# Modulation accumulated by one VectorE instruction per block, row norms with only the power on GpSimd

## Chip, core and metric

The kernel runs on one core of a Trainium2 chip. A core has a TensorE (PE in the profile, with its weight loads as PEld), a VectorE (DVE), a ScalarE (ACT), a GpSimd (POOL), and a SyncE (SP) that here issues nearly all DMAs. Each engine runs its own instructions in order and waits for the others at semaphores. The metric is the time of one execution in microseconds (us). Besides the reported time, the profile of one execution gives its span, from the first to the last instruction.

## The reference, cut to what matters

A sequence of 512 rows of width 1024, in float32, passes through two transformer blocks of two layers each. What the change touches in the second block is the norm around every sublayer and the modulation of that norm by a vector `c`:

```python
def rms_norm_2(x, g): x * rsqrt(mean(x*x) + 1e-6) * g

def sandwich(x, c_act, sublayer, g_pre, g_post, w_mod, b_mod):
    shift, scale, gate = split(c_act @ w_mod + b_mod, 3)      # w_mod is 1024 x 3072
    h = rms_norm_2(x, g_pre) * (1 + scale) + shift
    return x + gate * rms_norm_2(sublayer(h), g_post)
```

`sandwich` is applied four times (even mixer, MLP, odd mixer, MLP). The modulation `c_act @ w_mod` doesn't depend on `x`, so it can be computed at any time before its first use.

## The kernel before

Rows lie on 128 partitions, as four tiles (t = 0 to 3) of 128 rows. Dense products are taken in three fp32r matmuls each, high part by high part, low by high, high by low. For that every weight block of 128x1024 is split when it has arrived: ACT writes `whi`, DVE writes `wlo` = `raw` - `whi`. Activations are turned on TensorE (products with `ident`) and split likewise into `fTh` (ACT) and `fTl` (DVE); the `fT` of a layer is what its first dense products read. Results land in eight PSUM banks (`bank`).

One program order per engine is written out by a planner in the kernel: class `Line` keeps a clock per engine with estimated costs, and `defer` puts a piece of work into a heap until the planner's clock says that its inputs are there. TensorE's own stream is written in the same pass, so where a matmul stands in TensorE's order depends on when the planner reckons its inputs ready. A matmul whose inputs come later than reckoned holds up all that stand behind it.

Three places matter here.

**The modulation** (`mod_open`, `mod_load`, `mod_step`, `mod_go`, `mod_finish`) is computed inside the convolution FFN of both layers of the first block. There are 12 sums (4 sublayers, 3 kinds), 6 in each layer, and each is built from 8 blocks of 128x1024 weights (`mraw`, loaded by SP). The first block of a sum is scaled by `cact` into `macc` on ACT. Each of the other 7 was scaled in place on ACT and added to `macc` on GpSimd. Then four short products with `ones` on TensorE sum `macc` over the partitions. Steps are handed out along the up projections, one or two for each block of up weights.

**The norms between sublayers.** `post_start` and `out_part` finish a sublayer: sum of squares on ACT, `rstd` on GpSimd (a multiply-add with the mean and epsilon, then a power of -0.5), and on DVE `xr` = `y` * `rstd` + `xr`. Then `pre` squares `xr` on ACT, takes `rstd` on GpSimd, and on DVE multiplies by `rstd` and `scB` and adds `shB`; the result is turned into the next `fT`. `ln_pre_start` is the same hand-over after the last FFN of the first block. There are four hand-overs with `pre`, of four tiles each, and four ends with `post_start`.

**The start**: `hybrid` loads the gate bias `bg` and halves it on DVE before anything else of the layer.

In the profile every instruction has the line of the helper that records it (L186), so rows are told apart by their tiles.

Of the kernel before, what the change touches and what calls it, by code (L numbers as in the profile page):

```python
# [12 lines left out]
F32 = mybir.dt.float32  # L13
# [290 lines left out]
class KB:  # L304
# [305 lines left out]
    def split(self, hi, lo, ps, scale=None):  # L610
# [5 lines left out]
        else:  # L616
            nc.scalar.activation(hi, ps, AF.Copy, scale=scale)
            nc.vector.scalar_tensor_tensor(lo, ps, scale, hi.bitcast(F32), op0=ALU.mult, op1=ALU.subtract)

    def rstd(self, var, n, mul, eps, tag="rstd", pool=False):  # L620

        nc = self.nc
        ve = self.small(n, tag + "v")
        if mul == 1.0:
            nc.vector.tensor_scalar_add(ve, var, eps)
        else:
            (nc.gpsimd if pool else nc.vector).tensor_scalar(ve, var, mul, eps, op0=ALU.mult, op1=ALU.add)
        r = self.small(n, tag)
        nc.gpsimd.tensor_tensor(r, ve, self.mhalf[:, :n], op=ALU.pow)
        return r  # L630
# [62 lines left out]
    def setup(self):  # L693
        nc, A = self.nc, self.A
        self.ident = self.cn.tile([P, P], F32, name="ident")
        if not self.planning:
            make_identity(self.tc.nc, self.ident)
        self.mhalf = self.cn.tile([P, 64], F32, name="mhalf")
        nc.vector.memset(self.mhalf, -0.5)
        self.xd = A["x"]  # L700

    def first_x(self):
# [62 lines left out]
    def probs_out(self, pool, u):  # L765


        nc, sh = self.nc, u.shared
        if not sh:
            sh["pt"] = [self.tile(pool, (P, u.wide // P, 2, P), f"pt{e}") for e in range(2)]  # L770
            sh["ev"] = Event(2, lambda: self.defer(0, pv, *sh["pt"]))
        for e in range(2):
            pp = self.ps((P, 4, P))
            self.transpose4(pp, [u.sc[e][:, b * P:b * P + P] for b in range(u.nkb)])
            pt = sh["pt"][e][:, :u.nkb, u.pr, :]
            if e == 0:
                nc.scalar.activation(pt, pp[:, :u.nkb, :], AF.Copy)
            else:
                nc.vector.tensor_copy(pt, pp[:, :u.nkb, :])
        u.read.set()  # L780

        def pv():
            po = self.ps((P, 2 * P))
            vc = slice(64 * u.kv, 64 * u.kv + 64)
            for b in range(u.nkb):
                for e in range(2):
                    nc.tensor.matmul(po[64 * e:64 * e + 64, :], lhsT=u.v[:, u.b0 + b, vc],
                                     rhs=sh["pt"][e][:, b, :, :].rearrange("p r q -> p (r q)"),
                                     start=b == 0, stop=b == u.nkb - 1)
            self.poll()  # L790
            sl, k = slice(u.i * P, u.i * P + P), 2 * u.kv
            self.split(u.br.h[:, k:k + 2, sl], u.br.l[:, k:k + 2, sl], po.rearrange("p (r q) -> p r q", r=2))

        sh["ev"].set()

# [55 lines left out]
    def launch(self, pool, unit, step, br, **kw):  # L851


        units, depth = [], kw["bufs"] // 2

        def start(n):
            if n >= depth and not units[n - depth].read.done:
                units[n - depth].read.after(lambda: self.defer(0, lambda: start(n)))
                return
            unit(pool, units[n])  # L860

        for n in range(16):
            kv, i, pr = n // 8, n // 2 % 4, n % 2
            u = Unit(kv=kv, i=i, pr=pr, shared={} if pr == 0 else units[-1].shared, br=br, read=Event(),
                     **{k: v for k, v in kw.items() if k != "band"})
            u.b0, u.nkb, u.add = kw["band"](i)
            units.append(u)
            self.defer(n * step, lambda n=n: start(n), kw["kh"], kw["kl"])


    def hybrid(self, l, xT):
        nc, A = self.nc, self.A
        with self.pool("hp") as hp:
            W = Weights(self, "w_in", l)
            WB = Weights(self, "w_branch", l)
            bg = self.load(hp, A["b_gate"][l], (P, 24), "bg")
            nc.vector.tensor_scalar_mul(bg, bg, 0.5)
            mg = self.tile(hp, (P, KD, S), "mg")

            def branch(n, br, first, done=None):  # L880
# [20 lines left out]
            brc = new_br()  # L901
            with self.pool("cp") as cp:
                self.branch_c(cp, l, xT, W, brc)
                self.flush()
            bra = new_br()
            with self.pool("ap") as ap, ExitStack() as es:
# [361 lines left out]
    def mod_open(self, pool, end):  # L1268
        self.mod_pool, self.mod_raw, self.mod_end = pool, {}, end
        self.mod_left = Event((end - self.mod_n) // KD)  # L1270
        for j in range(2):
            self.mod_load(self.mod_n + j)

    def mod_load(self, i):
        if i < self.mod_end:
            s, kind, k = self.mod_steps[i]
            raw = self.tile(self.mod_pool, (P, D), "mraw", 3)
            o = (kind * KD + k) * P * D
            self.nc.sync.dma_start(raw, self.A["mod_w"][s][o:o + P * D].rearrange("(p c) -> p c", p=P))
            self.mod_raw[i] = raw  # L1280
# [8 lines left out]
    def mod_go(self):  # L1289
        nc, i = self.nc, self.mod_todo[0]  # L1290
        if not self.planning and nc.ready(self.mod_raw[i]) > self.now():
            self.defer(0, self.mod_go, self.mod_raw[i])
            return
        self.mod_todo.pop(0)
        s, kind, k = self.mod_steps[i]
        self.mod_load(i + 2)
        raw = self.mod_raw.pop(i)
        ck = self.cact[:, k:k + 1]
        if k == 0:
            self.mod_acc = self.tile(self.mod_pool, (P, D), "macc", 2)  # L1300
            nc.scalar.activation(self.mod_acc, raw, AF.Copy, scale=ck)
        else:
            nc.scalar.activation(raw, raw, AF.Copy, scale=ck)
            nc.gpsimd.tensor_tensor(self.mod_acc, self.mod_acc, raw, op=ALU.add)
        if k == KD - 1:
            acc, row = self.mod_acc, self.mod_sums[kind][s]

            def sums():
                ps = self.ps()
                for j in range(4):  # L1310
                    self.mm(ps[32 * j:32 * j + 32, 0:256], self.ones[:, 0:32], acc[:, 256 * j:256 * j + 256], 256)
                r = self.tile(self.mod_pool, (P, 256), "msum", 2)
                nc.scalar.activation(r, ps[:, 0:256], AF.Copy)
                nc.sync.dma_start(row.rearrange("(j c) -> j c", j=4), r[0:128:32, :])
                if c_last:
                    self.mod_finish(self.mod_pool)
                self.mod_left.set()

            c_last = i == len(self.mod_steps) - 1
            self.defer(0, sums, acc)  # L1320
# [12 lines left out]


    def open_pre(self, pool, s):
        self.shB = self.bcast(pool, self.mod_rows[0][s], D, "shB", 1, self.nc.sync)
        self.scB = self.bcast(pool, self.mod_rows[1][s], D, "scB", 1, self.nc.sync)

    def pre(self, t, x, h, fT, done=None):

        nc, scB, shB = self.nc, self.scB, self.shB
        ss = self.small(1, "ss1")
        nc.scalar.activation(h, x, AF.Square, accum_out=ss)

        def root():
            r = self.rstd(ss, 1, 1.0 / D, RMS_EPS, pool=True)
            self.defer(0, lambda: scale(r), r)

        def scale(r):
            nc.vector.scalar_tensor_tensor(h, x, r, scB, op0=ALU.mult, op1=ALU.mult)  # L1350
            nc.vector.tensor_tensor(h, h, shB, op=ALU.add)
            if done:
                done.set()
            self.defer_turn(t, h, fT)

        self.defer(0, root, ss)

    def open_post(self, s):
        bp = self.open_right()
# [4 lines left out]
    def out_part(self, t, n, ps, first, last):  # L1364
# [6 lines left out]
            nc.vector.tensor_tensor(y, y, ps, op=ALU.add)  # L1371
        if last:
            ss, gB = self.yss[:, t, n:n + 1], self.gB[:, 512 * n:512 * n + 512]
            nc.scalar.activation(ps, y, AF.Square, accum_out=ss)
            self.defer(0, lambda: nc.vector.tensor_tensor(y, y, gB, op=ALU.mult), ss)

    def post_start(self, s, out):
# [19 lines left out]
        def after(t):  # L1397
            if t > 1:
                self.wait(scaled[t - 2], True)
            y, xr = y4[:, t, :], xrs[t]  # L1400
            ss = self.small(1, "ss1")
            nc.vector.tensor_tensor(ss, self.yss[:, t, 0:1], self.yss[:, t, 1:2], op=ALU.add)
            r = self.rstd(ss, 1, 1.0 / D, RMS_EPS, pool=True)

            def scale():
                nc.vector.scalar_tensor_tensor(xr, y, r, xr, op0=ALU.mult, op1=ALU.add)
# [329 lines left out]
    def diff(self, dp, hT, W, v, yT):  # L1736
        nc, A = self.nc, self.A
        sub = self.load(dp, A["e_diff_norm"], (P, 1), "sub")
        nc.vector.tensor_scalar_mul(sub, sub, 1.0 - LAM_INIT)

        def head(h):
            T = self.tile(dp, (P, 512), "T", 2)
            self.toeplitz(T, h, 0, 512)
            qk = []
            shared = {}

            def unit(i):
# [3 lines left out]
                for m in range(2):  # L1751
# [3 lines left out]
                    nc.vector.tensor_tensor_reduce(s, ps[:, :Wd], T[:, 384 - i * P:512], 1.0, NEG,  # L1755
                                                   ALU.add, ALU.max, mx[:, m:m + 1])
                    s2.append(s)
                nc.vector.tensor_scalar_mul(nm_, mx, -1.0)
                for m in range(2):
                    nc.scalar.activation(s2[m], s2[m], AF.Exp, bias=nm_[:, m:m + 1], accum_out=sums[:, m:m + 1])  # L1760
# [49 lines left out]
            def ev(i, ps):  # L1810
                t = self.tile(dp, (P, 2, S), f"qk{i}", 2, F32R)
                qk.append(t)
                if i == 0:
                    self.stack_q([t[:, e, :] for e in range(2)], ps, HD ** -0.5)
                else:
                    qk.append(self.tile(dp, (P, 2, S), "qkl", 1, F32R))
                    self.stack_k(t, qk[2], ps)
                    for n in range(NT):
# [295 lines left out]
```

## Time and profile before

| | |
|---|---|
| median of 3 runs | 3478.86 us (3476.7 to 3480.21) |
| the profiled execution | 3478.01 us, span 3476.2 us |
| TensorE busy | 3366.9 us, 97% of the span |
| VectorE, ScalarE, GpSimd busy | 2078.5, 1433.7, 347.3 us |

Busy time alone tells little here: TensorE is busy nearly all the time, so what can change the total is what keeps it idle, and the level of its clock. A row of the chain of waits names the engine and tile that were waited for, the total in us, how often, and the longest. [...]

### The profile page before, as it was taken

The numbers are of one execution on the slowest core, as the hardware profiler recorded it, in microseconds if no ns is written. First come the engines' busy times: TensorE is split into PE (matmuls) and PEld (weight loads), VectorE is DVE, ScalarE is ACT, GpSimd is POOL, SyncE is SP. The second block draws the span as 40 slices with busy tenths as digits, with TensorE's granted clock in tenths as the row PEclk, the third lists the DMA queues.
The fourth block names the chain that finished last, engine by engine and source line by source line (L and its number), as shares of the span: only waits on it lengthen the run. The fifth ranks groups of instructions, "written<-read, shape, count | busy, mean of one in ns | idle before, by whom it ended". The sixth has DMA issues, their size and how long they took to land. (4 is left out here: it accounts for less than half of the span.)

```text
span 3476.2 us, 42309 instructions
## 1 busy us (share of the span) xinstructions
PE 3366.9 (97%) x16500; PEld 2749.0 (79%) x16500; DVE 2078.5 (60%) x3370; ACT 1433.7 (41%) x2497; POOL 347.3 (10%) x250
## 2 busy tenths in 40 slices
PE   8999999999999999999999899999999999999999
PEld 6887887777778878887777678777888887888887
DVE  5767467665667674676656666487433466553334
ACT  3544334544335452444543343475332344433222
POOL 0010001432200100013322000001000010010000
PEclk9999999999999999999999999999999999999999
DMA  4221445644332224445443221313322331333222
GB/s 147 70 69 60 143 155 181 207 164 145 118 118 70 72 67 140 158 177 182 162 153 118 86 79 55 100 49 136 104 97 97 121 111 55 103 138 109 93 95 87
DMA packets 116760, 399.24 MB, mean 115 GB/s; under 512 B 14608, under 2 KB 18592, under 8 KB 116560
## 3 DMA queue, kind: packets, MB, share of 16 engines
q1 hardware_dynamic: 115984, 394.44, 33.4%
q8 instruction: 130, 2.13, 0.2%
q0 software_dynamic: 576, 2.10, 0.2%
q14 instruction: 70, 0.57, 0.1%
HBM read 375.39 MB, written 23.71 MB: 115 GB/s over the span
## 5 line engine op out<-in xcount | busy, mean ns | idle before, releaser
L186 DVE TENSOR_TENSOR wlo<-raw,whi 128x1024 fp32r<-128x1024 f32 x531 | 716.5, 1354 | 688.5 <-ACT whi L186 678.4
L186 PE MATMUL bank<-fTh,whi 128*128 128x512 f32 (+1 forms) x2320 | 886.8, 382 | 0.0
L186 PE MATMUL bank<-fTl,whi 128*128 128x512 f32 (+1 forms) x2320 | 872.4, 376 | 0.4
L186 PE MATMUL bank<-fTh,wlo 128*128 128x512 f32 (+1 forms) x2320 | 871.8, 376 | 0.1
L186 ACT ACTIVATE whi<-raw 128x1024 fp32r<-128x1024 f32 x531 | 553.6, 1047 | 379.2 <-PE bank L186 345.8
L186 PEld LDWEIGHTS bank<-fTh,whi 128*128 128x128 f32 x2320 | 441.4, 190 | 90.5 <-issue 10.5
L186 PEld LDWEIGHTS bank<-fTh,wlo 128*128 128x128 f32 x2320 | 441.0, 190 | 85.4 <-DVE wlo L186 0.5
L186 PEld LDWEIGHTS bank<-fTl,whi 128*128 128x128 f32 x2320 | 441.5, 190 | 79.8 <-DVE fTl L186 1.3
L186 PE MATMUL bank<-whi,gh 128*128 128x512 f32 x864 | 343.2, 397 | 0.0
L186 PE MATMUL bank<-whi,gl 128*128 128x512 f32 x864 | 342.5, 396 | 0.0
L186 PE MATMUL bank<-wlo,gh 128*128 128x512 f32 x864 | 342.4, 396 | 0.0
L186 POOL TENSOR_TENSOR macc<-macc,mraw 128x1024 f32<-128x1024 f32 x84 | 225.9, 2690 | 449.2 <-ACT mraw L186 448.0
L186 PE MATMUL bank<-whi,fTh 128*128 128x512 f32 (+2 forms) x608 | 231.5, 381 | 12.8 <-ACT whi L186 7.1
L186 PE MATMUL bank<-wlo,fTh 128*128 128x512 f32 (+2 forms) x608 | 224.1, 369 | 9.9 <-DVE wlo L186 9.9
L186 PE MATMUL bank<-whi,fTl 128*128 128x512 f32 (+2 forms) x608 | 223.7, 368 | 0.5 <-DVE fTl L186 0.5
L186 PEld LDWEIGHTS bank<-whi,gh 128*128 128x128 f32 x864 | 163.1, 189 | 40.1 <-issue 0.8
L186 PEld LDWEIGHTS bank<-wlo,gh 128*128 128x128 f32 x864 | 163.2, 189 | 39.4
L186 PEld LDWEIGHTS bank<-whi,gl 128*128 128x128 f32 x864 | 162.9, 188 | 39.5
L186 POOL TENSOR_TENSOR rstd<-rstdv,mhalf 128x1 f32<-128x1 f32 x68 | 56.5, 832 | 1053.1 <-DVE rstdv L186 1050.5
L186 DVE SCALAR_TENSOR_TENSOR y<-bank,cv,y 128x511 f32<-128x511 f32 x176 | 131.3, 747 | 37.2 <-ACT y L186 34.1
L186 PEld LDWEIGHTS bank<-whi,fTh 128*128 128x128 f32 x608 | 115.9, 191 | 33.7 <-ACT whi L186 8.8
L186 PEld LDWEIGHTS bank<-wlo,fTh 128*128 128x128 f32 x608 | 116.0, 191 | 29.7 <-DVE wlo L186 12.3
(322 smaller groups left out, 4649.4 us busy)
## 6 DMA issues: line engine op xcount, KB each, us to landing
raw<-in_mlp_w_dram SPq DMA_DIRECT2D x128, 512.0 KB, 3.3
mraw<-in_mod_w_dram SPq DMA_DIRECT2D x96, 512.0 KB, 4.7
raw<-in_w_in_dram SPq DMA_DIRECT2D x88, 512.0 KB, 3.3
raw<-in_f_w_up_dram SPq DMA_DIRECT2D x88, 512.0 KB, 4.2
raw<-in_e_w_in_dram SPq DMA_DIRECT2D x48, 512.0 KB, 4.1
raw<-in_f_w_down_dram SPq DMA_DIRECT2D x40, 512.0 KB, 3.5
raw<-in_o_w_in_dram SPq DMA_DIRECT2D x30, 512.0 KB, 4.3
raw<-in_w_branch_dram SPq DMA_DIRECT2D x24, 512.0 KB, 3.3
```

Source lines behind the costliest of these rows:

```text
L186: r = f(*a, **k)
```

## The change

Six edits. (1) Each of the 84 later blocks of the modulation is one DVE instruction, `macc` = `mraw` * `cact` + `macc`; its scaling on ACT and its addition on GpSimd go. (2) The ring of `mraw` has 2 places instead of 3, and one block is loaded ahead instead of two. (3) In the norms, 1/1024 is folded into the square on ACT, epsilon is added on ACT (in `pre`) or in the DVE sum (in `post_start`), and GpSimd keeps only the power. In `pre` the product with `scB` goes ahead of the power, one DVE instruction is left behind it, and the squares have a tile of their own. (4) `bg` is halved after the first branch. (5) An attention unit writes its turned probabilities only when the product of the pair before has been put into the program. (6) A head of the differential attention waits, in program order, until all units of the head before are out.

```diff
+    def root(self, ve, tag="rstd"):
+        r = self.small(1, tag)
+        self.nc.gpsimd.tensor_tensor(r, ve, self.mhalf[:, :1], op=ALU.pow)
+        return r
...
+        if not u.before.done:
+            u.before.after(lambda: self.defer(0, lambda: self.probs_out(pool, u)))
+            return
...
             bg = self.load(hp, A["b_gate"][l], (P, 24), "bg")
-            nc.vector.tensor_scalar_mul(bg, bg, 0.5)
...
                 self.branch_c(cp, l, xT, W, brc)
+                nc.vector.tensor_scalar_mul(bg, bg, 0.5)
...
-        for j in range(2):
-            self.mod_load(self.mod_n + j)
+        self.mod_load(self.mod_n)
...
-            raw = self.tile(self.mod_pool, (P, D), "mraw", 3)
+            raw = self.tile(self.mod_pool, (P, D), "mraw", 2)
...
-        self.mod_load(i + 2)
+        self.mod_load(i + 1)
...
-            nc.scalar.activation(raw, raw, AF.Copy, scale=ck)
-            nc.gpsimd.tensor_tensor(self.mod_acc, self.mod_acc, raw, op=ALU.add)
+            nc.vector.scalar_tensor_tensor(self.mod_acc, raw, ck, self.mod_acc, op0=ALU.mult, op1=ALU.add)
...
-        ss = self.small(1, "ss1")
-        nc.scalar.activation(h, x, AF.Square, accum_out=ss)
-
-        def root():
-            r = self.rstd(ss, 1, 1.0 / D, RMS_EPS, pool=True)
-            self.defer(0, lambda: scale(r), r)
-
-        def scale(r):
-            nc.vector.scalar_tensor_tensor(h, x, r, scB, op0=ALU.mult, op1=ALU.mult)
-            nc.vector.tensor_tensor(h, h, shB, op=ALU.add)
+        ss, ve = self.small(1, "ss1"), self.small(1, "rstdv")
+        nc.scalar.activation(self.sq, x, AF.Square, scale=D ** -0.5, accum_out=ss)
+        nc.scalar.activation(ve, ss, AF.Identity, bias=self.reps)
+        nc.vector.tensor_tensor(h, x, scB, op=ALU.mult)
+
+        def scale():
+            nc.vector.scalar_tensor_tensor(h, h, r, shB, op0=ALU.mult, op1=ALU.add)
...
-        self.defer(0, root, ss)
+        r = self.root(ve)
+        self.defer(0, scale, r, h)
...
-            nc.scalar.activation(ps, y, AF.Square, accum_out=ss)
+            nc.scalar.activation(ps, y, AF.Square, scale=D ** -0.5, accum_out=ss)
...
-            ss = self.small(1, "ss1")
-            nc.vector.tensor_tensor(ss, self.yss[:, t, 0:1], self.yss[:, t, 1:2], op=ALU.add)
-            r = self.rstd(ss, 1, 1.0 / D, RMS_EPS, pool=True)
+            ss = self.small(1, "rstdv")
+            nc.vector.scalar_tensor_tensor(ss, self.yss[:, t, 0:1], RMS_EPS, self.yss[:, t, 1:2], op0=ALU.add, op1=ALU.add)
+            r = self.root(ss)
...
                 else:
+                    self.wait(before)
                     qk.append(self.tile(dp, (P, 2, S), "qkl", 1, F32R))
```

How the orders of the engines move is shown at three places. First, TensorE at the first of the 12 sums, in the first layer's FFN. Before, the four products on `macc` stand here:

```order
2761 L186 MATMUL bank_1109_5613<-fTh_4854,whi_5493 128x512
2762 L186 MATMUL bank_1109_5613<-fTl_4855,whi_5493 128x512
2763 L186 MATMUL bank_1109_5613<-fTh_4854,wlo_5494 128x512
2764 L186 MATMUL bank_1115_5646<-macc_5269,ones 32x256 x4
2765 L186 MATMUL bank_1109_5613<-fTh_4854,whi_5493 128x512
2766 L186 MATMUL bank_1109_5613<-fTl_4855,whi_5493 128x512
2767 L186 MATMUL bank_1109_5613<-fTh_4854,wlo_5494 128x512
```

Now the same sum stands 63 rows further down, at row 2827; row 2790 is the last matmul into `bank_1111`, which DVE reads:

```order
2788 L186 MATMUL bank_1111_5636<-fTh_4856,whi_5540 128x512
2789 L186 MATMUL bank_1111_5636<-fTl_4857,whi_5540 128x512
2790 L186 MATMUL bank_1111_5636<-fTh_4856,wlo_5541 128x512
2791 L186 MATMUL bank_1119_5680<-fTh_4856,whi_5587 128x512
2792 L186 MATMUL bank_1119_5680<-fTl_4857,whi_5587 128x512
```

```order
2825 L186 MATMUL bank_1125_5719<-fTl_4857,whi_5623 128x512
2826 L186 MATMUL bank_1125_5719<-fTh_4856,wlo_5624 128x512
2827 L186 MATMUL bank_1126_5732<-macc_5269,ones 32x256 x4
2828 L186 MATMUL bank_1125_5719<-fTh_4856,whi_5623 128x512
2829 L186 MATMUL bank_1125_5719<-fTl_4857,whi_5623 128x512
```

And this is what DVE does ahead of that sum now; row 724 waits for `bank_1111`, and row 726 completes the sum:

```order
720 L186 TENSOR_TENSOR wlo_5647<-raw_5544,whi_5646 128x1024
721 L186 TENSOR_TENSOR y_1110_5632<-y_1104_5593,y_1110_5632 128x512
722 L186 TENSOR_TENSOR gl_5660<-y_1110_5632,gh_5659 128x512
723 L186 SCALAR_TENSOR_TENSOR macc_5269<-mraw_5614,cact,macc_5269 128x1024
724 L186 SCALAR_TENSOR_TENSOR y_1118_5675<-bank_1111_5636,cv_5078,y_1118_5675 128x511 x2
725 L186 TENSOR_TENSOR wlo_5694<-raw_5591,whi_5693 128x1024
726 L186 SCALAR_TENSOR_TENSOR macc_5269<-mraw_5663,cact,macc_5269 128x1024
```

The sum moved from row 2764 to row 2827, and 36 TensorE rows lie between the last bank that DVE needs ahead of row 726 and the sum. Of the 12 sums ten moved down so, by 12 to 159 rows, and two moved up, by 9 rows each.

Second, DVE at the start of the program. Before:

```order
3 L186 TENSOR_TENSOR cact<-c_81,th_83 128x8
4 L186 MEMSET ones 128x128
5 L186 TENSOR_SCALAR bg_114<-bg_114 128x24
6 L186 TENSOR_TENSOR fTl_93<-bank_25_133,fTh_92 128x4x128
7 L186 TENSOR_TENSOR fTl_93<-bank_26_140,fTh_92 128x4x128
8 L186 TENSOR_TENSOR wlo_148<-raw_99,whi_147 128x1024
```

Now:

```order
4 L186 TENSOR_TENSOR cact<-c_83,th_85 128x8
5 L186 MEMSET ones 128x128
6 L186 TENSOR_TENSOR fTl_95<-bank_25_134,fTh_94 128x4x128
7 L186 TENSOR_TENSOR fTl_95<-bank_26_141,fTh_94 128x4x128
8 L186 TENSOR_TENSOR wlo_149<-raw_101,whi_148 128x1024
9 L186 TENSOR_TENSOR fTl_95<-bank_30_157,fTh_94 128x4x128
```

The instruction on `bg` that stood ahead of the first `fTl` and `wlo` is gone from there; it comes at the end of the first branch.

Third, the hand-over from the first MLP to the odd mixer. GpSimd before, where `ss_4282` and `ss_4289` are the sums of `pre` of tiles 0 and 1, and the other `ss` those of `post_start`:

```order
205 L186 TENSOR_SCALAR rstdv_22415<-ss_4278_22413 128x1
206 L186 TENSOR_TENSOR rstd_22417<-rstdv_22415,mhalf 128x1
207 L186 TENSOR_SCALAR rstdv_22453<-ss_4283_22451 128x1
208 L186 TENSOR_TENSOR rstd_22455<-rstdv_22453,mhalf 128x1
209 L186 TENSOR_SCALAR rstdv_22464<-ss_4282_22444 128x1
210 L186 TENSOR_TENSOR rstd_22466<-rstdv_22464,mhalf 128x1
211 L186 TENSOR_SCALAR rstdv_22499<-ss_4291_22497 128x1
212 L186 TENSOR_TENSOR rstd_22501<-rstdv_22499,mhalf 128x1
```

ACT now, where `sq` is the square in `pre` (of tiles 1 and 2 here), `yss` the squares of `out_part`, and `fTh` the evacuation of turned tile 0:

```order
1538 L186 ACTIVATE bank_4279_22330,yss_20299<-y_20298 128x512
1539 L186 ACTIVATE sq_22144,ss_4287_22393<-xr_22142 128x1024
1540 L186 ACTIVATE rstdv_22394<-ss_4287_22393,reps 128x1
1541 L186 ACTIVATE fTh_22149<-bank_4290_22403 128x4x128
1542 L186 ACTIVATE fTh_22149<-bank_4291_22410 128x4x128
1543 L186 ACTIVATE bank_4285_22371,yss_20299<-y_20298 128x512
1544 L186 ACTIVATE sq_22144,ss_4296_22460<-xr_22382 128x1024
```

On GpSimd every pair became one instruction. On ACT the square of tile 1 stands ahead of the evacuation of tile 0, and that of tile 2 behind it.

## Rows read from the trace of the kernel before

**Rows 1.** The chain of waits of TensorE over the whole span, longest first.

```profile
PE bank L186 <- POOL macc L186: 36.5, 12, 5.1
PE bank L186 <- DVE ss L186: 14.1, 3, 4.8
...
PE bank L186 <- ACT fTh L186: 5.7, 1, 5.7
```

**Rows 2.** Stretches: the two FFN stretches with modulation, and one of an MLP.

```profile
582.00:903.00 321.00, 303.08 (x1316) 240.88 (x1314) 205.11 (x187) 154.85 (x186) 112.78 (x42) 0.97 0.52 179
1530.00:1852.00 322.00, 303.76 (x1322) 241.69 (x1320) 204.00 (x185) 155.06 (x186) 112.85 (x42) 0.97 0.49 170
2610.00:2697.00 87.00, 87.00 (x375) 70.00 (x374) 35.36 (x40) 25.89 (x32) 0.00 (x0) 1.00 0.28 97
```

**Rows 3.** Timeline of TensorE at the first sum: start, us, instruction.

```profile
623.57 0.64 PE L186 MATMUL bank<-macc,ones 128*32 128x256 f32 x8 [3.22 <-POOL macc L186]
...
626.01 0.63 PE L186 MATMUL bank<-fTl,whi 128*128 128x512 f32 x1
```

**Rows 4.** Stretches behind the longer waits, first and last of eight.

```profile
623.50:627.70 4.20, 4.13 (x17) 3.03 (x18) 1.69 (x2) 4.20 (x6) 0.02 (x1) 0.59 0.50 163
...
1851.40:1856.50 5.10, 5.04 (x21) 3.71 (x22) 2.50 (x3) 0.39 (x1) 0.01 (x1) 0.67 0.26 77
```

**Rows 5.** DVE groups, 582 to 903 us: busy, mean ns | idle before.

```profile
L186 DVE TENSOR_TENSOR wlo<-raw,whi 128x1024 fp32r<-128x1024 f32 (+1 forms) x55 | 104.1, 1894 | 69.5 <-ACT whi L186 66.3 <-DMA mraw<-in_mod_w_dram 3.0
L186 DVE SCALAR_TENSOR_TENSOR y<-bank,cv,y 128x511 f32<-128x511 f32 x76 | 56.7, 747 | 9.5 <-ACT y L186 8.1
L186 DVE TENSOR_TENSOR y<-y,y 128x512 f32<-128x512 f32 x19 | 24.0, 1263 | 0.0
```

**Rows 6.** The same in an MLP (2610 to 2697 us).

```profile
L186 DVE TENSOR_TENSOR wlo<-raw,whi 128x1024 fp32r<-128x1024 f32 x16 | 19.6, 1225 | 34.4 <-ACT whi L186 34.3
L186 DVE TENSOR_TENSOR gl<-r,gh 128x512 fp32r<-128x512 f32 x8 | 5.5, 692 | 5.6 <-ACT gh L186 5.6
...
L186 DVE TENSOR_TENSOR r<-r 128x512 f32<-128x512 f32 x8 | 5.5, 684 | 0.0
```

**Rows 7.** Groups of the whole span.

```profile
L186 POOL TENSOR_TENSOR macc<-macc,mraw 128x1024 f32<-128x1024 f32 x84 | 225.9, 2690 | 449.2 <-ACT mraw L186 448.0
...
L186 ACT ACTIVATE mraw<-mraw,cact 128x1024 f32<-128x1024 f32 x84 | 94.9, 1138 | 0.0
...
L186 DVE SCALAR_TENSOR_TENSOR y<-y,rstd,gb 128x1024 f32<-128x1024 f32 x20 | 25.7, 1285 | 3.8 <-POOL rstd L186 2.2
...
L186 DVE TENSOR_TENSOR y<-y,shB 128x1024 f32<-128x1024 f32 x16 | 19.6, 1225 | 0.6
```

**Rows 8.** The loads of the modulation weights (its tile), from issue to landing.

```profile
DMA to landing us min/median/max: 3.3/4.7/7.7
```

**Rows 9.** Timeline of the start, DVE and TensorE.

```profile
13.44 0.18 DVE L186 TENSOR_SCALAR bg<-bg 128x24 f32<-128x24 f32 x1 [10.32 <-DMA bg<-in_b_gate_dram]
...
14.73 1.21 DVE L186 TENSOR_TENSOR wlo<-raw,whi 128x1024 fp32r<-128x1024 f32 x1
...
9.12 0.80 PE L186 MATMUL bank<-whi,fTh 128*128 128x512 f32 x1 [1.63 <-ACT whi L186]
16.00 0.80 PE L186 MATMUL bank<-wlo,fTh 128*128 128x512 f32 x1 [6.08 <-DVE wlo L186]
...
24.25 0.50 PE L186 MATMUL bank<-wlo,fTh 128*128 128x512 f32 x1 [0.76 <-DVE wlo L186]
```

**Rows 10.** Timeline at a hand-over: TensorE, and DVE for the last tile.

```profile
2802.48 1.94 PE L186 MATMUL bank<-ident,y 128*128 128x128 f32 x8 [4.85 <-DVE ss L186]
...
2816.08 1.23 DVE L186 TENSOR_TENSOR y<-y,shB 128x1024 f32<-128x1024 f32 x1
```

**Rows 11.** The stretch behind that wait.

```profile
2802.40:2809.00 6.60, 6.38 (x29) 5.88 (x30) 5.17 (x6) 3.20 (x5) 2.61 (x5) 0.52 0.40 155
```

**Rows 12.** Timeline of the end, GpSimd.

```profile
3469.98 0.56 POOL L186 TENSOR_SCALAR rstdv<-ss 128x1 f32<-128x1 f32 x1 [4.41 <-DVE ss L186]
```

More of the change, by code (lines that the diff above doesn't have):

```diff
@@ L699, in setup @@
         nc.vector.memset(self.mhalf, -0.5)
+        self.reps = self.cn.tile([P, 1], F32, name="reps")
+        nc.vector.memset(self.reps, RMS_EPS)
         self.xd = A["x"]
@@ L792, in pv @@
             self.split(u.br.h[:, k:k + 2, sl], u.br.l[:, k:k + 2, sl], po.rearrange("p (r q) -> p r q", r=2))
+            u.over.set()
         sh["ev"].set()
@@ L865, in launch @@
                      **{k: v for k, v in kw.items() if k != "band"})
+            u.before, u.over = (units[-1].before, units[-1].over) if pr else (units[-1].over if units else Event(0), Event())
             u.b0, u.nkb, u.add = kw["band"](i)
@@ L1335, in open_pre @@
     def open_pre(self, pool, s):
+        self.sq = self.tile(pool, (P, D), "sq")
         self.shB = self.bcast(pool, self.mod_rows[0][s], D, "shB", 1, self.nc.sync)
@@ L1739, in diff @@
         nc.vector.tensor_scalar_mul(sub, sub, 1.0 - LAM_INIT)
+        scored = [Event(0)]
         def head(h):
             T = self.tile(dp, (P, 512), "T", 2)
+            before, now = scored[-1], Event(NT)
+            scored.append(now)
             self.toeplitz(T, h, 0, 512)
@@ L1757, in unit @@
                     s2.append(s)
+                now.set()
                 nc.vector.tensor_scalar_mul(nm_, mx, -1.0)
```

## Prediction

> **What bounds the kernel now.** TensorE is busy 97% of the span, so I first asked where it stands still, and only then what the others do. The chain of waits of TensorE [rows 1] is led by the modulation: 36.5 us in 12 waits for `macc` on GpSimd, one for each of the 12 sums. Next come three waits of 4.6 to 4.9 us and one of 5.7 us at the four hand-overs between sublayers. The reader is to see in the stretches [rows 2] that this is the right place: in the two FFN stretches TensorE is idle 17.9 and 18.2 us, nearly all of it those 12 waits, while in an MLP it is idle 0.0 of 87 us and gets through 375 matmuls, 0.232 us each.
>
> A wait costs more than itself. [...] Eight of the 12 waits are over 3 us and are followed by such a stretch [rows 4]. Length times (1 - clock), over the eight, is 17.3 us (1.7 in the first, 1.7 in the last). The modulation thus costs TensorE 36.5 + 17.3 = 53.8 us.
>
> Why is the sum late? GpSimd's addition takes 2.69 us [rows 7], and DVE suffers while it runs: `wlo` takes 1.894 us in the FFN [rows 5] and 1.225 us in an MLP where GpSimd is idle [rows 6]; the square `y`*`y`, the same operation as `r`*`r`, takes 1.263 against 0.684. ACT's scaling of `mraw` stands in order behind work that waits for that DVE, and the addition behind the scaling.
>
> **The change, part by part.**
>
> *Accumulation.* 84 additions on GpSimd (226 us) and 84 scalings on ACT (95 us) go. Neither is a gain by itself: TensorE doesn't wait for either engine's total, only for the last addition of each sum. DVE gets 84 instructions that the trace doesn't have; the nearest row has the same form, two float32 tiles of 128x1024 and one scalar per partition: 1.285 us [rows 7]. That is 108 us more. DVE gets back the slowdown: per layer 55 x (1.894 - 1.225) + 19 x (1.263 - 0.684) = 48 us, about 96 us in both. So DVE is loaded as before, within some 12 us.
>
> Does the sum still wait? In the new order 36 TensorE rows lie between the last bank that DVE needs and the first sum: 36 x 0.232 = 8.4 us. In them DVE does two convolution steps (2 x 0.747), a `wlo` (1.225) and the accumulation (1.285), 4.0 us, with about 0.8 us of ACT ahead. Done for all 12 sums, room exceeds work by 0.7 to 3 us. Queues on ACT and DVE can eat that, so I leave 0.35 us on average per sum, 4.2 us, and no stretch at the low clock (the waits under 1 us today, four of the 12, have none). Gain: 53.8 - 4.2 = 49.6 us. Bounds: 53.8, and 27 if half stays.
>
> [...]
>
> *One load ahead.* A block of `mraw` lands 4.7 us after its issue (median; 3.3 to 7.7) [rows 8]. SP issues it behind a weight load, which waits for a `wlo` three blocks back; from that `wlo` to the accumulation DVE has 5 to 8 instructions in most steps, about 6 us. So the load mostly hides; cost 0. If that cover is gone, DVE stands at the accumulation, and behind it `wlo` and the convolutions. The next weights have 50 TensorE rows (11.6 us) of lead at least, so TensorE doesn't feel one such wait. It feels them if they recur: one up block gives TensorE 24 rows, 5.57 us, and DVE 1.225 + 2 x 0.747 + (0.684 + 0.692)/2 + 1.09 x 1.285 = 4.8 us. About 0.7 us per step is free.
>
> *The gate bias.* DVE stands at `bg` until 13.44 us, and `wlo` ends at 15.9; TensorE waits 6.08 us for it [rows 9]. Without it `wlo` can end 1.2 us after ACT's half, which released TensorE at 9.12: at 10.3. But what follows is a chain through ACT and DVE for the next three tiles, which the new order puts between the products; today it is done by 24.25. I take half the wait, 3 us; bounds 0 and 6.
>
> *Norms.* In `pre` the multiply-add on GpSimd (0.56 us) and one DVE instruction (1.225) leave the chain behind the square, 1.8 us per tile; ACT's addition of epsilon costs less than the 0.56 it replaces. DVE's total is unchanged. Does TensorE gain? Before, a hand-over costs 4.85 us of wait [rows 10] and 6.6 x 0.48 = 3.2 us of clock [rows 11]. Walking the new order with these durations, tile 1's wait goes. But ACT works in order, and the square of tile 1 stands ahead of the evacuation of tile 0, that of tile 2 ahead of tile 1's; so `fT` of tile 1 is late next, by about 3 us. The last tile's norm, which ends at 2817.3 now [rows 10], ends about 4 us earlier; but its turn stands 27 to 51 rows of half width earlier in TensorE's order, 3 to 6 us, and TensorE waits there. I take 0 for the four hand-overs; bounds: 14.1 + 5.7 us of waits and 3 x 3.2 us of clock gained (29), 2.5 us lost at each (10). At the very end nothing hides the 0.56 us on GpSimd [rows 12]: gain 0.6.
>
> *Attention.* Both edits only shift program order. The differential attention keeps TensorE's order row for row. In the sink and dense units a turn moves some 8 matmuls down, with dense products in its place; if those ran out, it would cost about 1 us a pair. I take 0.
>
> **Sum.** 49.6 + 3 + 0.6 + 0 = 53.2 us. The profiled execution took 3478.0 us, 0.9 under the median: 3424.8, or 3426 us against the median of 3478.9.
>
> **Rivals.**
>
> *The sum waits for DVE instead.* If ACT and DVE lag as far behind the planner as now, half of the 53.8 stays: 26.9 + 3.6 gives 3448 us. For it: the planner is what put the sums too early. Against: the room above, and that GpSimd's hold on DVE is gone.
>
> *The hand-overs shrink too.* If the waits there vanish altogether, 29 us more: 3397 us. For it: 1.8 us per tile. Against: in-order ACT.
>
> *DVE becomes the bound: slower.* The place is the accumulation standing for its load. It costs nothing up to 0.7 us per step; the gain of 53 us is used up at 0.7 + 53/84 = 1.33 us. At 2.0 us, a landing of 6.7 us, it loses 84 x 1.3 = 109: 3535 us. For it: one load ahead instead of two, and 7.7 us seen. Against: the median.
>
> *Accumulation at half rate.* If the instruction takes 2 x 1.225 us, DVE lacks 1.17 - 0.7 us per step, 40 us: 3466 us. The rows show no such form. [...]
>
> *No effect.* If the time at the sums comes back elsewhere in the FFN, as waits for `wlo` for instance, the time stays at 3478 us.
>
> **Chances.** Forecast 0.70, sum waits 0.11, hand-overs 0.08, half rate 0.02, no effect 0.04, slower 0.05. Some 0.2% is what timing this kernel can tell from no change. Faster has 0.70 + 0.11 + 0.08 + 0.02 = 0.91, same 0.04, slower 0.05. The forecast's own range is 3404 to 3444 (hand-overs -10 to +14, start, residual waits). With the first two rivals it is 3396 to 3452.
>
> **What would show it.** Right: no waits of TensorE for `macc` over 1 us, a granted clock of 1.00 in both FFN stretches, each some 27 us shorter; `wlo` there at 1.2 us; the accumulation at 1.29 us; first `wlo` by 11 us. Wrong: TensorE waiting for `macc` on DVE, DVE idle for `mraw` loads, or an accumulation above 2 us; hand-overs whose TensorE idle time changes by more than 5 us each.

## The result, and the profile after

The changed kernel takes 3417.65 us (median of 4 runs, 3415.09 to 3419.69), the one before 3477.78 in the same comparison: a ratio of 0.9827, with a 95% interval of 0.981 to 0.9844. That is 60 us or 1.7% faster. The forecast was 3426 us with a range of its own of 3404 to 3444, and of 3396 to 3452 together with the first two rivals. The profiled execution took 3418.77 us with a span of 3416.7, against 3476.2: 59.5 us less.

The first view is the chain of waits of TensorE, engine and tile waited for, then us in total, times, longest:

```profile
PE bank L186 <- DVE y L186: 17.1, 8, 3.9
PE bank L186 <- ACT fTh L186: 10.2, 4, 4.2
PE bank L186 <- ACT whi L186: 7.5, 4, 3.1
PE bank L186 <- DVE wlo L186: 6.5, 9, 2.2
```

The row that led the list before, 36.5 us for `macc` [rows 1], is gone; no row names `macc` any more. The three waits for `ss` at the hand-overs are gone too, but waits for `fTh` and for `y` have grown where they were. (The profile names `ss` because it came last; what the turn reads is `y`, and at [rows 10] the addition of `shB` to it ends 0.15 us ahead of the turn.)

The second view is the stretches that answer to [rows 2], the two FFN stretches and one of an MLP (in these rows as in [rows 2, 4, 11]: from:to, length, busy time and instructions of PE, PEld, DVE, ACT, POOL, then the granted clock as a share of full speed, the busy share of the DMA engines, GB/s):

```profile
578.00:899.00 321.00, 321.00 (x1424) 256.18 (x1423) 221.51 (x249) 124.99 (x158) 0.00 (x0) 1.00 0.54 187
1499.20:1820.00 320.80, 320.80 (x1426) 257.18 (x1425) 220.78 (x249) 123.96 (x157) 0.00 (x0) 1.00 0.52 181
2560.00:2647.00 87.00, 87.00 (x375) 70.00 (x374) 33.04 (x39) 24.73 (x31) 0.00 (x0) 1.00 0.28 91
```

Stretches of the same length now hold 1424 matmuls instead of 1316, TensorE is never idle in them, and the granted clock is 1.00 instead of 0.97. The third view says what VectorE does in the first of them:

```profile
L186 DVE TENSOR_TENSOR wlo<-raw,whi 128x1024 fp32r<-128x1024 f32 (+1 forms) x60 | 71.6, 1196 | 50.4 <-ACT whi L186 50.0
...
L186 DVE SCALAR_TENSOR_TENSOR macc<-mraw,cact,macc 128x1024 f32<-128x1024 f32 x42 | 53.7, 1278 | 0.0
L186 DVE TENSOR_TENSOR y<-y,y 128x512 f32<-128x512 f32 x22 | 15.1, 685 | 0.0
```

`wlo` went from 1894 to 1196 ns and the product `y`*`y` from 1263 to 685 [rows 5]; the new accumulation takes 1278 ns. So VectorE was given 84 instructions and its total over the span is the same, 2080.1 us against 2078.5.

One sign that the prediction named for being wrong did show: VectorE stands for `mraw`. The group of the accumulation over the whole span:

```profile
L186 DVE SCALAR_TENSOR_TENSOR macc<-mraw,cact,macc 128x1024 f32<-128x1024 f32 x84 | 107.4, 1278 | 4.3 <-DMA mraw<-in_mod_w_dram 4.2
```

These are 4.2 us in four waits of 0.5 to 2.0 us, all in the second FFN, where TensorE is idle 0.0 us. So they cost nothing.

The start, as the timeline of TensorE shows it (start, us, instruction, idle time before it and who ended it):

```profile
8.61 0.80 PE L186 MATMUL bank<-whi,fTh 128*128 128x512 f32 x1 [1.63 <-ACT whi L186]
9.87 0.80 PE L186 MATMUL bank<-wlo,fTh 128*128 128x512 f32 x1 [0.47 <-DVE wlo L186]
```

The 6.08 us for the first `wlo` [rows 9] are 0.47. The load of `x`, with which both traces begin, also ended 0.5 us earlier here (at 5.04 us, before at 5.55).

The hand-over from the first MLP to the odd mixer, which was [rows 10], on TensorE and on ACT:

```profile
2742.27 0.38 PE L186 MATMUL bank<-fTh,whi 128*128 128x256 f32 x1 [2.18 <-ACT fTh L186]
...
2753.94 1.06 PE L186 MATMUL bank<-ident,y 128*128 128x128 f32 x8 [3.88 <-DVE y L186]
```

```profile
2740.20 1.06 ACT L186 ACTIVATE sq<-xr 128x1024 f32<-128x1024 f32 x1 [3.40 <-DVE xr L186]
2741.16 0.19 ACT L186 ACTIVATION_READ_ACCUMULATOR sq<-xr 128x1 f32 x1
2741.44 0.29 ACT L186 ACTIVATE rstdv<-ss,reps 128x1 f32<-128x1 f32 x1
2741.64 1.06 ACT L186 ACTIVATE fTh<-bank 128x512 fp32r<-128x512 f32 x2
```

One wait of 4.85 us became two, 2.18 for tile 1's `fTh` and 3.88 for the turn of the last tile. ACT's rows say why the first is there: the square of tile 2, its read-out and the addition of epsilon stand ahead of the evacuation of tile 1, 1.44 us.

To see where the 59.5 us are, I took, at the same number of finished matmuls in both traces (16500 in all), the difference of the times, good to some 0.4 us: -4.0 us when the FFN of the first layer begins, -31.1 at the first matmuls of the second layer, -30.9 ahead of its FFN, -57.9 at its end, -56.7 behind the first hand-over, -57.1 ahead of the second and -58.6 behind it, -58.6 and -58.6 at the third, -58.9 and -58.3 at the fourth, -59.5 at the end. The chain of waits of before has also a wait of 1.61 us for `wlo` at the start of the second layer (0.35 now): `bg` is halved in each layer, and the prediction counted only the first. So the modulation is 27.1 - 1.3 + 27.0 = 52.8 us, the gate bias 4.0 + 1.3 = 5.3, and all the rest 1.4. About 1 us of that rest comes in the last MLP, where TensorE waits in neither trace; its cause stays open.

### The profile page after: what moved, and what is told of

Its sections match the earlier page's. It is cut to its first block, busy times and chain, and to the rows that moved or that the text cites. A ratio compares the mean times of both kernels' runs of the same rounds, so it can differ in the third digit from the quotient of the medians.

```text
span 3416.7 us, 42049 instructions
## 1 busy us (share of the span) xinstructions
PE 3346.6 (98%) x16500; PEld 2734.5 (80%) x16500; DVE 2080.1 (61%) x3455; ACT 1354.7 (40%) x2427; POOL 109.6 (3%) x134
## 5 line engine op out<-in xcount | busy, mean ns | idle before, releaser
L186 DVE TENSOR_TENSOR wlo<-raw,whi 128x1024 fp32r<-128x1024 f32 x531 | 642.1, 1214 | 640.0 <-ACT whi L186 634.9
L186 DVE SCALAR_TENSOR_TENSOR y<-bank,cv,y 128x511 f32<-128x511 f32 x176 | 131.8, 749 | 52.7 <-ACT y L186 49.6
L186 POOL TENSOR_TENSOR rstd<-rstdv,mhalf 128x1 f32<-128x1 f32 x68 | 64.3, 945 | 2544.8 <-DVE rstdv L186 2482.3
L186 PEld LDWEIGHTS bank<-whi,fTl 128*128 128x128 f32 x608 | 116.0, 191 | 20.3 <-DVE fTl L186 0.4
```

The lines of the kernel that those rows point to most:

```text
L186: r = f(*a, **k)
```

## Experiments

Each kernel is compared with the kernel before, timed beside it on the same chip. Kernels that were not timed together are compared by these ratios, since the median of the kernel before moved from 3474.7 to 3478.4 us. The interval of a ratio is some 4.5 us to either side, so that a smaller difference between two kernels rests on their traces and not on the times.

**The modulation by itself.** The kernel before with edits 1 and 2 alone.

> The kernel before with edits 1 and 2 alone (accumulation in one VectorE instruction per block, ring of two). My theory, that the modulation carries the gain and norms give nothing: 54 us less than before, about 3424 us, with no wait of TensorE for macc and a granted clock of 1.00 in both FFN stretches. Rival, that the norms or the start carry a part of what looks like the modulation's gain: above 3435 us.

Measured: 3423.6 us, ratio 0.9844 (0.9831 to 0.9858). TensorE waits for `macc` nowhere. At equal numbers of matmuls 25.6 us are gone behind the first FFN, 27.0 more at the end of the second, and 1.8 more in the stretch behind that. The rival is out: the modulation carries some 54 of the 60 us.

**Is it the engine, or the place?** Here nothing moves to VectorE; the planner only hands the sums out later.

```diff
-            self.defer(0, sums, acc)
+            self.defer(0, lambda: self.defer(8.0, sums), acc)
```

> The kernel before, with scaling on ScalarE and addition on GpSimd as they were; only the planner hands out each of the 12 sums 8 us later. If the cause of the 54 us is where the sum stood in TensorE's order: the waits for macc go, 45 to 54 us less, 3424 to 3433 us, although GpSimd still takes 2.3 to 3.1 us per addition and still slows VectorE. Rival, GpSimd's hold on VectorE costs TensorE by itself: the waits for macc go, but TensorE waits for wlo, gh or y in the FFN instead, and the time is above 3450 us.

Measured: 3426.0 us, ratio 0.9849 (0.9836 to 0.9863), the same as `mod_only`. The stretches and VectorE's groups of this kernel:

```profile
582.00:850.00 268.00, 267.27 (x1187) 213.65 (x1186) 180.07 (x166) 136.02 (x163) 95.32 (x36) 1.00 0.57 194
1530.00:1800.00 270.00, 270.00 (x1185) 215.25 (x1184) 180.37 (x165) 136.13 (x163) 99.59 (x37) 1.00 0.50 178
```

```profile
L186 DVE TENSOR_TENSOR wlo<-raw,whi 128x1024 fp32r<-128x1024 f32 (+1 forms) x50 | 91.9, 1841 | 51.6 <-ACT whi L186 49.3 <-DMA ms<-msum 2.0
...
L186 DVE TENSOR_TENSOR y<-y,y 128x512 f32<-128x512 f32 x16 | 19.7, 1230 | 0.0
```

GpSimd is busy for 95 us of 268, `wlo` still takes 1.84 us, and yet TensorE is idle for 0.73 us in all (one wait for `macc`, at 665) and the clock is 1.00. So GpSimd's hold on VectorE costs TensorE nothing by itself, and the slow addition costs nothing where the sums stand late enough. What cost 54 us was that the sums stood in TensorE's order ahead of the time at which they were ready.

The other remedy is enough as well. `mod_ring3` below is the kernel before with edit 1 alone, and its 12 sums stand within 15 rows up and 12 rows down of where they stood before, by the matmuls ahead of them. The fourth stands at the same count in both, 3833. Before, and with edit 1:

```profile
779.79 1.08 PE L186 MATMUL bank<-macc,ones 128*32 128x256 f32 x8 [4.84 <-POOL macc L186]
```

```profile
762.24 0.64 PE L186 MATMUL bank<-macc,ones 128*32 128x256 f32 x8
```

None of its sums waits, and they have 0.56 to 1.23 us of room. So the faster accumulation makes the old places right, and later places make the old accumulation do; either takes 48 us or more of the 54 by the ratios. The move of ten sums further down, which the changed kernel and `mod_only` share, came with edit 2 and wasn't needed. Why the planner's places fit the new instruction is a reading, not tested: its table has 1.20 us for it, 1.278 measured, where GpSimd's addition was estimated at 2.30 and took 2.69, and VectorE's slowing beside it (`wlo` at 1.894 us instead of 1.196) wasn't in the table at all.

**How much does VectorE have left?** A second instruction behind each accumulation, hidden from the planner. (Nobody reads what it writes.)

```diff
+            e = nc if self.planning else nc.nc
+            e.vector.tensor_tensor(raw, raw, self.mod_acc, op=ALU.add)
```

> The changed kernel with a second VectorE instruction of 1.2 us behind each of the 84 accumulations (it adds the sum onto the used block; nobody reads that), of which the planner isn't told, so that the orders stay as they are. The prediction's account of an up block, 0.7 us free per step: (1.23 - 0.7) x 84 = 44 us more, about 3462 us. Rival, by the trace after, VectorE is idle 99.5 us in the 42 steps of an FFN stretch, 2.4 us per step: the blocks lose nothing, and only the sums, which had 0.4 to 1.6 us of room, wait now: 0 to 12 us more, 3418 to 3430 us.

Measured: 3449.3 us, ratio 0.9922 (0.9908 to 0.9935), 31 to 33 us more than the changed kernel, between the two. The instruction takes 1225 ns, 103 us in all. TensorE's chain of waits shows where the cost is, and that it is not in the blocks:

```profile
PE bank L186 <- DVE macc L186: 21.3, 11, 4.0
```

No wait for `wlo` appeared in the FFN. VectorE has the time, so my 0.7 us per step was too little; but the last accumulation of a sum now ends later, and 11 sums, which had only 0.4 to 1.6 us of room between it and TensorE, wait 1.9 us each. The rest is the clock: its mean over the span is 0.992 instead of 0.995, 10 us. I had put the price of the waits too low (0 to 12 us).

**One load ahead or two.** `mod_only` with three places and two loads ahead.

> mod_only with three places for mraw and two loads ahead, as before the change. The prediction's step that one load ahead costs nothing: 3421 to 3426 us, as mod_only (3423.6). Rival, the shorter cover costs a part of the 84 steps: 3418 us or less.

Measured: 3426.5 us, ratio 0.9862 (0.9849 to 0.9876). No gain from the longer cover; the interval overlaps that of `mod_only`. The test is not clean, since the sums stand elsewhere too (as said above), but the traces agree: VectorE's waits for `mraw` are 1.8 us here and 4.1 in `mod_only`, and TensorE waits for `macc` in neither.

**The norms undone.**

> The changed kernel with the norms of before (edit 3 undone in pre, out_part and post_start). My theory: the norms gain nothing at the four hand-overs and 0.6 us at the end, so 3416 to 3422 us, with 4.6 to 5.7 us of wait back at each hand-over in one piece. Rival, the shorter chain counts by 1.8 us per tile: 3430 us or more.

Measured: 3419.7 us (3418.35 to 3422.3), ratio 0.983 (0.9816 to 0.9843). By matmul counts the new norms lose 1.3 us at the first hand-over and gain 1.6 at the second, 0.2 at the third, lose 0.7 at the fourth and gain 1.3 behind it: 1.1 us together, which is less than the times can tell.

**The last turn given out later.** The changed kernel with one line different.

```diff
-            self.defer_turn(t, h, fT)
+            self.defer(4.0 if t == NT - 1 else 0, lambda: self.defer_turn(t, h, fT), h)
```

> The changed kernel, with the turn of the last tile at each of the four hand-overs given out 4 us later by the planner (all else as it is). If TensorE stands in front of that turn because the planner reckons its input too early, as with the sums: the two waits of 3.9 us at the third and fourth hand-over go with the low clock behind them, 8 to 11 us less than the changed kernel, 3407 to 3410 us; at the first two the turn moves by 3 and 9 rows only, and 0 to 3 us go there. Rival, the tile is simply late and the wait moves behind the turn to the second half of the first products: no change, 3418 us.

Measured: 3408.9 us (3407.55 to 3415.48), ratio 0.9804 (0.979 to 0.9817), 8 to 9 us less than the changed kernel by ratio and median. The stretch behind the turn that waited 3.88 us has a granted clock of 1.00 (0.81 with the wait):

```profile
2745.00:2755.00 10.00, 9.35 (x79) 9.15 (x79) 7.97 (x9) 6.01 (x10) 0.55 (x1) 1.00 0.58 195
```

By matmul counts 3.9 us went at the first hand-over, 1 at the second, 3.2 at the third and 2.8 at the fourth. So the total is as expected, but by luck: the third and fourth gave 6.0 us instead of 8 to 11, and the first gave more than the 0 to 3 us left for the first two. At the third and fourth VectorE finishes the tile as late as it did, and it is the cause of the sums once more: a row that stands too early in TensorE's order, with other work behind it. At the first the planner also changed VectorE's order. There the norm of the last tile now goes ahead of two evacuations into `fTl`, and its `y` is ready 2.2 us earlier; three rows alone would not have removed a wait of 3.79 us.

**The same with the old norms.**

> The norms of before (as in norms_old) and the late turn of the last tile (as in late_turn), all else as changed. If the new norms are worth something only where the planner gives the last turn out late: no gain of the late turn here, since with the old norms TensorE stands at the turn of tile 1 for the sum of squares (4.6 to 4.9 us), behind which nothing else is left to do: 3417 to 3421 us. Rival, the late turn alone is the gain whatever the norms: 3409 to 3412 us.

Measured: 3422.2 us, ratio 0.9846 (0.9832 to 0.9859): no gain, as the first theory had it. With the old norms TensorE waits at the turn of tile 1, and what stands behind that turn are the first products, which take tiles 0 and 1 together (256 columns):

```profile
2747.38 1.94 PE L186 MATMUL bank<-ident,y 128*128 128x128 f32 x8 [4.86 <-DVE ss L186]
```

The three waits of 4.6 to 4.9 us are as they were in `norms_old`. So the shorter chain of the new norms is real, and is worth something only together with the order.

**ScalarE's order at the hand-over.** `late_turn`, with both calls of `pre` put off by 1 us in the planner.

```diff
-                self.pre(t, x, y[:, t, :], fT, scaled[t])
+                self.defer(1.0, lambda: self.pre(t, x, y[:, t, :], fT, scaled[t]), x)
...
-                    self.pre(t, xr, y, fT, scaled[t])
+                    self.defer(1.0, lambda: self.pre(t, xr, y, fT, scaled[t]), xr)
```

> late_turn, with the square and the product with scB of each tile given out 1 us later by the planner, so that on ScalarE the evacuation of turned tile 1 stands ahead of the square of tile 2 (and, in most hand-overs, that of tile 0 ahead of the square of tile 1). If in-order ScalarE is what makes the first products wait for fTh: the 4.2, 2.2 and 3.1 us at the second to fourth hand-over shrink to about 1 us each, with some of the low clock behind them, 6 to 8 us less than late_turn, 3401 to 3403 us. Rival, the wait only changes its name, because the square that now comes later makes tile 2 or 3 late: 3406 to 3412 us.

Measured: 3402.3 us (3398.5 to 3402.94), ratio 0.9785 (0.9772 to 0.9798): 6.6 us less than `late_turn` by the ratios, 75 us less than before, and the fastest kernel of this study. ACT at the third hand-over now, the evacuation of tile 1 and the square of tile 2:

```profile
2730.69 1.09 ACT L186 ACTIVATE fTh<-bank 128x512 fp32r<-128x512 f32 x2 [2.75 <-PE bank L186]
...
2733.87 1.05 ACT L186 ACTIVATE sq<-xr 128x1024 f32<-128x1024 f32 x1
```

The evacuation no longer stands behind the square. TensorE's waits for `fTh` fell from 10.2 to 2.7 us. At the second hand-over the square of tile 2 still stands ahead of tile 1's evacuation, and 2.1 us of wait for `fTh` stayed with it. A part of the wait did change its name, as the rival had it: turns now wait 1.2 to 2.1 us at each hand-over. Nor did the gain come only where it was expected: by matmul counts some 2.8 us went at the first hand-over, which the expectation had not counted (there TensorE waited for `whi` and `wlo`, not for `fTh`), 0.9 at the second, 2.3 at the third and 0.5 at the fourth.

**The gate bias first again.**

> The changed kernel with the gate bias halved first, as before (edit 4 undone). By the trace after, the start was 4.0 us shorter by the third wait: 3421 to 3422.5 us with the wait of 6.1 us for wlo back. Rival, the load of x that both traces begin with differs by 0.5 us and is part of the 4.0: 3420 to 3421 us.

Measured: 3424.2 us (3421.7 to 3426.72), ratio 0.9851 (0.9838 to 0.9864); 5 to 8 us more than the changed kernel by spans (3421.8 against 3416.7) and by ratios. The waits for `wlo` are back in both layers, 5.97 us at 15.41 and 1.61 at 947.58. Both expectations were a little low, since they too forgot the second layer (1.3 us). The load of `x` is not part of it: it ends at the same time in this trace and in that of the changed kernel (5.08 and 5.04 us), and the changed kernel is 4.0 us ahead when the first FFN begins. But that place varies. The traces of the eight kernels with the late `bg` and the old cost table are 2.2 to 4.0 us ahead of before there, and the other four between 0.7 behind and 0.4 ahead.

**The attention edits undone.**

> The changed kernel without the two edits of program order in the attentions (edits 5 and 6). The prediction's step that they cost and gain nothing: 3415 to 3420 us. Rival, the turn of probabilities that they push down was a wait that is hidden now: 3422 us or more.

Measured: 3419.3 us (3416.04 to 3421.41), ratio 0.9842 (0.9828 to 0.9855). That is 5 us more than the changed kernel by the ratios and 2.7 less by the spans of the traces, so no difference that the times can tell. The waits of TensorE for the turned probabilities (`pt`) are 0.7 us here and 0.8 with the edits. This agrees with the prediction's 0, though a cost or gain of a few us isn't ruled out.

**Better estimates everywhere.** If single wrong estimates cost so much, a truer table should pay. It doesn't follow.

```diff
-            return (0.13 if op == "scalar_tensor_tensor" else 0.07) + n / 960
+            return (0.21 if op == "scalar_tensor_tensor" else 0.16) + n / 960
...
-            return 0.03 + n / 1120 + 0.08 * max(0, len(ins) + len(outs) - 2)
-        return 0.07 + n / 460 if n > 64 else 0.62
+            return 0.15 + n / 1138 + 0.2 * (len(outs) - 1)
+        return 0.07 + n / 460 if n > 64 else 1.45
```

> The changed kernel with nothing but the planner's cost table moved to what the trace shows: VectorE 0.16 (scalar-tensor-tensor 0.21) us more than its elements, ScalarE 0.15 and 0.2 for a sum beside, a one-column instruction on GpSimd 1.45 us. No delay is given by hand. If wrong estimates are the cause of the waits at the hand-overs, the gain is that of late_turn (the last turn moves down by 21 to 24 rows at the third and fourth hand-over, the square of the next tile stays ahead of fTh on ScalarE): 3406 to 3412 us. Rival, the turns of the first tiles, which move down by up to 30 rows too, cost as much as is gained: 3416 to 3422 us.

Measured: 3482.9 us, ratio 1.0025 (1.0014 to 1.0035): both theories missed, by 65 us. The loss is spread over the program, not at the hand-overs alone:

```profile
PE bank L186 <- DVE wlo L186: 24.4, 25, 3.8
PE bank L186 <- ACT whi L186: 14.0, 6, 6.4
...
PE bank L186 <- DVE macc L186: 6.9, 1, 6.9
```

Weights are late in 31 places instead of 13, and one sum waits 6.9 us. Of the 65 us against the changed kernel 11 are lost between 200 and 300 us, 6 from 460 to 560, 8 from 1000 to 1200 and 8 in the second FFN. The new table moves rows all over the program, and TensorE then meets, among others, weights that aren't split yet (24 us more of waits for `wlo` and `whi`). Which of the four numbers does it, and why the split of the weights falls behind, stays open.

**GpSimd's power by itself.** One execution, with the second half's product with `gB` behind the power.

> The changed kernel, with the second half's product with gB in the ends of the sublayers moved behind the power (it takes rstd as its scalar, so VectorE runs nothing beside the power at the end of the program). Looked at for one row: if GpSimd's one-column instruction waits out a VectorE instruction that reads two tiles in SBUF, the power at the very end takes 0.55 us instead of 0.86. Rival, the power takes longer there for another reason (the first of its kind after a pause, for instance): it stays at 0.86 us. The time is not at issue; the end has 0.4 to 0.5 us more of VectorE in its chain.

The last power of the changed kernel, and of this one:

```profile
3410.78 0.86 POOL L186 TENSOR_TENSOR rstd<-rstdv,mhalf 128x1 f32<-128x1 f32 x1 [4.71 <-DVE rstdv L186]
```

```profile
3413.93 0.55 POOL L186 TENSOR_TENSOR rstd<-rstdv,mhalf 128x1 f32<-128x1 f32 x1 [5.02 <-DVE rstdv L186]
```

0.55 us, as the first theory says, and so it is in all four powers at the end.

## Why the prediction was right, step by step

*The modulation, 49.6 us.* Measured 52.8 in place, 54 alone. The mechanism was right: no wait for `macc`, clock 1.00, the accumulation at 1.278 us. Of the 52.8 us, 36.5 were the waits themselves [rows 1]; that leaves 16.3 for the lower clock behind them, which I had estimated at 17.3 over eight stretches (granted clock 0.59 in the first, behind a wait of 3.22 us [rows 3], and 0.67 in the last [rows 4]). The 4.2 us that I left for queues weren't needed; all 12 sums have room, 0.38 to 1.60 us of it, where I had worked out 0.7 to 3. This term is the largest part of what the forecast was short. What I had not seen is that the gain needs no new instruction: `sums_late` has it too. My reading of why the sum is late was true, but the remedy could have been one number in the planner. Nor did the gain need the room that I counted in the new order, 36 rows at the first sum: in `mod_ring3` the sums stand nearly where they did before and don't wait either.

*Half rate.* The accumulation of two float32 tiles takes 1.278 us, the product of two 1.225 [rows 7]. The 2 x 1.225 us of that rival didn't show.

*One load ahead, 0.* Right, within what the times tell (`mod_ring3`): VectorE does stand for `mraw`, 4.2 us in all, and TensorE doesn't feel it. *Attention, 0.* Not contradicted (`units_old`).

*The gate bias, 3 us.* Mis-sized: 5.3 between the two profiled executions. The wait went nearly whole (5.6 of 6.08 us, and 4.0 of that stayed a gain), where I had taken half; over eight traces 2.2 to 4.0 us stayed, so the 3 us were fair for the first layer. What the step surely had wrong is that it left out that `hybrid` runs twice, 1.3 us.

*The hand-overs, 0.* Right in the sum, which is a balance of losses and gains of up to 1.6 us, and at three of the four right in the mechanism: tile 1's wait went, and `fTh` of tile 1 was late next behind the square on ACT (2.2 to 4.2 us where I said about 3). The last turn, which stood earlier, waited 3.8 to 3.9 us at three of the four (I said 3 to 6); at the second it didn't wait. `sq_behind` and `late_turn` show the two new waits by taking them away, `norms_old` and `old_norms_late` the old one by bringing it back. The first hand-over went otherwise: before, TensorE waited 5.7 us there for `fTh`, and now it waits 3.1 us for `whi` and 2.2 for `wlo` ahead of the last turn, which I hadn't foreseen.

*The end, 0.6 us.* Mis-sized: from the last VectorE addition to `xr` it was 3.01 us and is 2.74, a gain of 0.27, because the power that stayed now takes 0.86 us instead of 0.55.

*The rival that VectorE becomes the bound.* Its price rested on 0.7 us free per step, and `acc_more` shows that the blocks have more; what is tight is the room ahead of the sums. Its sign, VectorE idle for `mraw`, came true without its cost.

## What to carry to other kernels

When an in-order engine waits, look first at what stands behind the waiting row: if there is other work, the row stands too early for its input, and moving it may be worth as much as making its input faster (here 3426.0 us against 3426.5 with the faster input in nearly the old places). A shorter chain pays only if the order lets the waiting engine use it, so change both together, and test them apart. An order that is tuned on wrong estimates is tuned to those estimates: correct the one that a wait points to, and measure, before correcting all.

## What the runs showed of the hardware

In the changed kernel the one-column power on GpSimd took longer where VectorE was running an instruction that reads two tiles, neither of them a bank. It took 0.55 us when VectorE read a bank beside it or did nothing, 0.86 to 0.99 beside such an instruction of 0.68 to 0.75 us, and 1.2 to 1.6 beside one of 1.2 to 1.3 (0.6 where only the end of one fell beside it, or one of 0.42 us did); beside all of these it ended about 0.4 us behind that instruction. At the third hand-over:

```profile
2728.80 1.28 DVE L186 SCALAR_TENSOR_TENSOR y<-y,rstd,shB 128x1024 f32<-128x1024 f32 x1
```

```profile
2728.99 1.50 POOL L186 TENSOR_TENSOR rstd<-rstdv,mhalf 128x1 f32<-128x1 f32 x1 [0.85 <-DVE rstdv L186]
```

In the kernel before, the multiply-add that the change took away [rows 12] took 0.56 us beside such a product of 0.68, and 0.19 where VectorE read a bank or stood still. So its 0.56 us were mostly a wait for VectorE, and the power inherited it: 0.86 us for the last one beside a product of 0.69, and 0.55 in `gb_behind`, where that product is gone from beside it.
